# Two output projections from eight products to seven, with operand sums kept in DRAM

## The chip, the core and the metric

The kernel runs on one core of one Trainium2 chip. The metric is device time in microseconds, the median of several runs. A core has TensorE (PE, matmuls; PEld is its weight load), VectorE (DVE), ScalarE (ACT), GpSimd (POOL) and SyncE (SP). DMAs are issued from the queues of SP, GpSimd and (once, here) ScalarE.

## The reference

One layer of a decoder block over x of 2048 tokens by 1024 channels, all in float32. Cut to what matters here:

```python
h = rms_norm(x, norm_g)
v_c, b_c, c_c, z_c, q, k, v, z_a, gate_logits = split(h @ w_in)      # 1024 -> 8704 columns
y_c = b_c * conv3(c_c * v_c) * silu(z_c)         # causal, depthwise, width 3
y_a = y_c @ w_conv_out                           # 1024 x 1024
o = sliding_window_attention(rms(q), rms(k), v, sinks) * silu(z_a)   # window 128, 16 heads, 4 kv heads
y_b = o @ w_attn_out                             # 1024 x 1024
g_a, g_b = split(sigmoid(gate_logits + gate_b))
out = x + (g_a * y_a + g_b * y_b) @ w_out        # 1024 x 1024
```

## The kernel before

**Layout and precision.** The work is done in two tiles of 1024 tokens (`NT` = 2, `T` = 1024), with channels on the partitions. Every float32 operand is split into a high part, rounded to the format that TensorE multiplies in, and a low part, the rest. The high part is a cast on ScalarE, the low part a subtraction on VectorE (`split`, L240, for operands; `two`, L308, for weights; VectorE's operations all carry L213, the line of the helper that issues them). A product of two operands takes three matmuls: high x high, high x low, low x high. A matmul has a 128 x 128 weight block and 512 columns.

**Seven products.** A unit is a block of 256 output columns over one tile. The inner dimension is halved (1024 channels as 4 pairs of chunks of 128), the tokens are halved (q = 0, 1) and the output columns are halved (i = 0, 1), so a unit is a 2 x 2 block product. `sunit` computes it with seven products in place of eight, with sums of weights and sums of operands formed beforehand, and a few sums of results afterwards. `product` (L412) issues one of the seven: 4 x 3 = 12 matmuls. The order is 1, 5, 6, 2, 7, 3, 4. Results gather in three PSUM banks, X, V and Y. Between products ScalarE copies X into Y and V into a spare buffer s5, and VectorE adds; then a function `fin` takes each of the four quarters away (gate, store, multiply).

**The operands.** The seven operands of the tile's h, in 4 chunks each, are 28 buffers of the pool `oppool`, which has just 28. All input projections use them: k, v, q, cv (the convolution's two inputs), b, the merge gates ga and gb, and the gates za and z. In the first tile k and v go another way, and the first q unit too.

**The two branch projections.** `ya_unit` and `yb_unit` did not use seven products. After z, 16 operands of the gated convolution output were split straight from SBUF (`opa`), and 16 of the gated attention output were loaded back from the DRAM tensor `ocd` (`ocr`, then `opb`). `mm_t` (L1154) multiplied them in the plain way: for each quarter of a unit 8 chunks x 3 matmuls. VectorE took a quarter from PSUM, multiplied it by the gate (`tha`, `thb`, loaded from `gd`) and stored it: ya's to `md`; yb's was added to `m`, loaded back from `md`, and the sum went to `mt`, from which the output projection loaded its operand as weights. During yb the operands of the next tile (`next_tile`), or of w_out (`wo_side`), were loaded, normalized, summed in SBUF and split.

**What sets the order.** Each engine's instructions run in the order in which they are recorded, by a hand-made clock of ticks: a tick is one product (12 matmuls, in the plain projection a half quarter). `put(n, f)` sets a step to be recorded at tick n; `run` goes through a unit product by product and records, at each tick, weight loads (`ahead_loads`), one piece of the next weights (`piece`) and the steps due. Weights: raw loads of 512 KB, up to four at once; their split forms take a ring of 8 buffers, of which a unit of seven products needs 7. Attention blocks (32 per tile) are placed by a list of ticks; each has steps from its loads at 5 ticks ahead to its sum at 15 ticks after. Small buffers of 128 x 512 come from a pool of 19 (`slot`), wider ones from a pool of 2 (`upool`).

Of the kernel before, what the change touches and what calls it, by code (L numbers as in the profile page):

```python
# [8 lines left out]
F32 = mybir.dt.float32  # L9
# [49 lines left out]


@with_exitstack
def block_kernel(
# [37 lines left out]
    def bank(name):  # L100
        return ps_x.tile([P, H], F32, tag="x", name=name)
# [16 lines left out]
    ocd = [dram.tile([KC, P, T], F32, name=f"ocd{t}") for t in range(NT)]  # L118
    yd = [dram.tile([KC, P, T], F32, name=f"yd{t}") for t in range(NT)]
    md = [dram.tile([KC, P, T], F32, name=f"md{t}") for t in range(NT)]  # L120
    mt = [dram.tile([KC, P, T], F32, name=f"mt{t}") for t in range(NT)]
# [132 lines left out]
    WRING, RAWS = 8, 4  # L254
    live, rawlive = [0], [0]

    def load_half(i=None):
# [16 lines left out]
        elif kind in "SP":  # L274
# [8 lines left out]
        else:  # L283
            raw = rawpool.tile([P, KP, UC], F32, tag="raw", name=name)
            w, c0 = srcs
            nc.sync.dma_start(raw, w[c0 // UC, h].rearrange("r (j c) -> r j c", c=UC))
# [12 lines left out]
    def pieces_of(n):  # L299
# [15 lines left out]
        if kind in "SP":  # L315
# [9 lines left out]
            def single():  # L325
                hl = wpool.tile([P, 2, KP, P], F32R, tag="w", name=f"{name}_d")
                w[4] = (hl[:, 0], hl[:, 1])
                return two(hl[:, 0], hl[:, 1], raws[2 * n + 1][:, 1])
# [19 lines left out]
            return w, [(2, 0, lambda: pair(0, 1, 2, "a")), (1, 0, single), (0, 0, sums),  # L348
                       (2, 1, lambda: of_sums(1, 5, 6, "s")), (2, 1, lambda: of_sums(0, 7, 3, "t"))]

        def part(p):
            hi, lo = (v.rearrange("p (j c) -> p j c", c=UC) for v in wpair(f"{name}_{p}"))
            w[p] = (hi, lo)
            return two(hi, lo, raws[2 * n + p])

        return w, [(2, 1, lambda: part(0)), (2, 1, lambda: part(1))]

    def open_prep():
# [3 lines left out]
        w, pieces = pieces_of(n)  # L362
        ready.append(w)
        todo.extend((n, i) + p for i, p in enumerate(pieces))
        return True

    def piece():
# [4 lines left out]
        need = [2 * n + i] if plan[n][0] in "TP" else [2 * n, 2 * n + 1][: 1 + min(i, 1)]  # L372
# [24 lines left out]
    Y = ps_y.tile([P, H], F32, tag="y", name="Y")  # L397
# [8 lines left out]
    def product(ps, u, n, ops, start):  # L406
# [11 lines left out]
        live[0] -= sum(c for m, c in USES if n in m and m <= d)  # L418
# [4 lines left out]
    def sunit(key, ops, fin, two=False):  # L423
# [34 lines left out]
    def qunit(key, ops, fin):  # L458
# [4 lines left out]
        for q in range(2):  # L463
            for i in range(2):
                ps = bank(f"Q{nm}_{i}_{q}")
# [545 lines left out]
    def att_values(t, j, b, pcv, v2):  # L1011
        xh, xl, y = pcv
        po = mbank(f"po{t}_{j}_{b}").rearrange("p g q -> p (g q)")
        for h in range(2):
            cs = slice(h * 2 * P, (h + 1) * 2 * P)
            for n, (kind, xx) in enumerate(((2 + h, xh), (h, y), (2 + h, xl))):
                nc.tensor.matmul(  # L1017
                    po[:, cs], lhsT=v2[:, kind, :], rhs=xx[:, :, h * HD : (h + 1) * HD],
                    start=n == 0, stop=n == 2)
# [89 lines left out]
    def fin_z(t, j, src, nm, use):  # L1109
        other = {}  # L1110

        def load():
            for i, q in ((0, 0), (1, 1), (0, 1), (1, 0)):
                o = slot([P, H], F32, f"{nm}in{t}_{j}_{i}_{q}")
                nc.sync.dma_start(o, src[2 * j + i, :, hs(q)])
                other[i, q] = o

        def fin(i, q, val):
# [7 lines left out]
            def last():  # L1126
                o = other[i, q]
                mul(o, o, s)
                use(k, q, o)
# [7 lines left out]
        return fin, load  # L1137

    def split_op(src, name):
        o = optile(name)  # L1140
        split(o[:, 0], o[:, 1], src)
        return o


    def mm_t(ps, u, half, opt, q, first, last):
        cs = slice(half * P, (half + 1) * P)

        for n, k in enumerate((0, 2, 4, 1, 3, 5, 6, 7) if first else (0, 2, 4, 6, 1, 3, 5, 7)):
            j, p = divmod(k, 2)
            force(u, p)  # L1150
            hi, lo = ready[u][p]
            o = opt[k, q]
            for i, (w, m) in enumerate(((hi, 0), (hi, 1), (lo, 0))):
                nc.tensor.matmul(  # L1154
                    ps, lhsT=w[:, j, cs], rhs=o[:, m, :],
                    start=n == 0 and i == 0, stop=n == KC - 1 and i == 2)
            if n == KP - 1:
                live[0] -= 2 * last
                yield
        live[0] -= 2 * last  # L1160

    def quarters(order):
        return [(hf, q) for q in order for hf in range(2)]

    def branch(t, key, j, opt, fin, order):
        u = unit((key, t, j))
        for n, (hf, q) in enumerate(quarters(order)):
            ps = bank(f"{key}{t}_{j}_{hf}_{q}")
            yield from mm_t(ps, u, hf, opt, q, (key, j) == ("ya", 0), n == 3)
            fin(2 * j + hf, q, ps)  # L1170
            yield

    def load(src, k, q, name):
        tl = slot([P, H], F32, name)
        nc.sync.dma_start(tl, src[k, :, hs(q)])
        return tl

    def ya_unit(t, j, opt, order):
        th = {}

        def get(n):
            for hf, q in quarters(order)[2 * n : 2 * n + 2]:
                k = 2 * j + hf
                th[k, q] = load(gd[t][0], k, q, f"tha{t}_{k}_{q}")

        def fin(k, q, ps):
            m = th[k, q]
            vec.scalar_tensor_tensor(
                out=m, in0=m, scalar=1.0, in1=ps, op0=ALU.add, op1=ALU.mult)
            nc.sync.dma_start(md[t][k, :, hs(q)], m)  # L1190

        return branch(t, "ya", j, opt, fin, order), get

    def yb_unit(t, j, opt, order):
        th, m1 = {}, {}

        def get(n):
            pair = upool.tile([P, 2 * H + 2], F32, tag="u", name=f"thb{t}_{j}_{n}")
            for i, (hf, q) in enumerate(quarters(order)[2 * n : 2 * n + 2]):
                k = 2 * j + hf  # L1200
                th[k, q] = pair[:, hs(i)]
                nc.sync.dma_start(th[k, q], gd[t][1][k, :, hs(q)])
                m1[k, q] = spare(f"m1{t}_{k}_{q}")
                nc.sync.dma_start(m1[k, q], md[t][k, :, hs(q)])

        def fin(k, q, ps):
            m = th[k, q]
            vec.scalar_tensor_tensor(
                out=m, in0=m, scalar=1.0, in1=ps, op0=ALU.add, op1=ALU.mult)
            add(m, m, m1[k, q])  # L1210
            nc.sync.dma_start(mt[t][k, :, hs(q)], m)

        return branch(t, "yb", j, opt, fin, order), get
# [22 lines left out]
    def wo_side(n0, st):  # L1236
        raw = st["raw"]

        def ld(c):
            for q in range(2):  # L1240
                h = raw[c, q] = slot([P, H], F32, f"wo_{c}_{q}")
                nc.gpsimd.dma_start(h, w_o[c * P : (c + 1) * P, hs(q)])  # L1242

        def sums(j):
# [445 lines left out]
```

## Time and profile before

| | |
|---|---|
| median of 3 runs | 1946.24 us (1945.74 to 1947.4) |
| profiled execution: span | 1944.5 us; its own time outside the trace is not given apart, and the median is 1.7 us above the span |
| PE busy, matmuls | 1929.3 us, 99%, 8846 |
| DVE busy | 1462.6 us, 75% |
| ACT busy | 937.8 us, 48% |
| POOL busy | 580.9 us, 30% |
| DMA | 366.54 MB, 189 GB/s over the span |

A share of busy time is a mean over stages with different limits. In the span, the first tile's projections and attention run to about 572 us, za and z to 729, ya to 816 and yb to 905; the second tile has the same stages up to 1788, and the output projection follows. The page's rows in tenths cut the span into 40 slices. The chain of waits goes back from the last instruction: at each step to what released it.

### The profile page before, as it was taken

How to read it: one execution, taken by the hardware profiler on the slowest of the kernel's cores; microseconds unless marked ns; L12 is line 12 of the kernel's file. 1: busy time of each engine (PE TensorE's matmuls, PEld its weight loads, DVE VectorE, ACT ScalarE, POOL GpSimd, SP SyncE). 2: the span in 40 equal slices, each digit the busy share in tenths (PEclk: the TensorE clock that was granted, in tenths of full speed). 3: DMA queues.
4: the chain of work that ended last, by engine and by line, in shares of the span. 5: the costliest groups of instructions: out<-in, count | busy, mean ns of one | idle time of the engine just before them, and what ended most of it. 6: DMA issues, size and time to landing. Idle time of an engine off the chain costs nothing.

```text
span 1944.5 us, 27473 instructions
## 1 busy us (share of the span) xinstructions
PE 1929.3 (99%) x8846; PEld 1602.0 (82%) x8846; DVE 1462.6 (75%) x2500; ACT 937.8 (48%) x1876; POOL 580.9 (30%) x826
## 2 busy tenths in 40 slices
PE   9999999999999999999999999999999999999999
PEld 7778888888888888888878888888888888888887
DVE  7999898888886564379689888888997664366654
ACT  7655455556664342224565544556675343222221
POOL 2361443445662000100462343445654000100000
PEclk9999999999999999999999999999999999999999
DMA  8485555577775435874585554577776435855453
GB/s 306 104 217 172 153 162 170 165 224 235 236 248 190 168 97 184 291 246 136 161 207 156 167 163 142 164 224 234 238 236 213 167 109 183 283 180 171 152 174 113
DMA packets 217375, 366.54 MB, mean 189 GB/s; under 512 B 29264, under 2 KB 104016, under 8 KB 217232
## 3 DMA queue, kind: packets, MB, share of 16 engines
q1 hardware_dynamic: 189696, 288.96, 46.8%
q0 software_dynamic: 27392, 75.80, 13.5%
q8 instruction: 70, 1.15, 0.2%
q14 instruction: 73, 0.60, 0.1%
q10 hardware_dynamic: 144, 0.03, 0.0%
HBM read 251.17 MB, written 113.51 MB: 188 GB/s over the span
## 4 chain that ended last, share of the span: by engine, by line
PE 86%; DVE 7%; DMA 3%; issue 2%; POOL 2%; ACT 1%; SPq 0%; DVEq 0%; POOLq 0%
PE Y L412 27%; PE yb L1154 9%; PE ya L1154 8%; PE Vcv L412 4%; PE Xcv L412 4%; PE Xgb L412 2%; PE Vgb L412 2%; PE Xza L412 2%; PE Vza L412 2%; PE Vga L412 2%; PE Xz L412 2%; PE Vo L412 2%; PE Xo L412 2%; PE po L1017 2%; PE Xga L412 2%
## 5 line engine op out<-in xcount | busy, mean ns | idle before, releaser
L979 POOL DMA_DIRECT2D x<-fd x256 | 139.6, 551 | 92.7 <-DMA fd<-f 57.5
L1000 POOL TENSOR_SCALAR_AFFINE_SELECT xh<-xh 64x512 fp32r<-64x512 f32 x64 | 72.9, 1140 | 139.4 <-DVE xl L213 122.8
L952 ACT ACTIVATE p<-s,st,rq 128x128 f32<-128x128 f32 x256 | 112.9, 450 | 0.0
L972 POOL DMA_DIRECT2D fd<-f x64 | 37.0, 578 | 246.6 <-DVE f L213 215.9
L213 DVE SCALAR_TENSOR_TENSOR tha<-tha,ya 128x512 f32<-128x512 f32 x32 | 22.0, 687 | 96.3 <-PE ya L1154 96.3
L1154 PE MATMUL ya<-opa,wya_1h 128*128 128x512 f32 x256 | 79.5, 391 | 0.9 <-ACT opa L240 0.5
L412 PE MATMUL Xcv<-oph,wcv_ah 128*128 128x512 f32 x256 | 79.5, 392 | 0.0
L1154 PE MATMUL yb<-opb,wyb_1h 128*128 128x512 f32 x256 | 78.9, 389 | 0.0
L1154 PE MATMUL yb<-opb,wyb_0h 128*128 128x512 f32 x256 | 78.9, 389 | 0.0
L1154 PE MATMUL ya<-opa,wya_0h 128*128 128x512 f32 x256 | 78.8, 389 | 0.0
L240 ACT CAST opb<-ocr 128x512 fp32r<-128x512 f32 x32 | 19.9, 621 | 111.3 <-DMA ocr<-ocd 106.0
L1000 POOL TENSOR_SCALAR_AFFINE_SELECT xl<-xl 64x512 fp32r<-64x512 f32 x64 | 68.6, 1072 | 4.4
L1242 POOL DMA_DIRECT2D wo<-in_w_out x16 | 8.7, 541 | 192.6 <-DVE opb L213 180.5
L521 POOL DMA_DIRECT2D x<-in_x x8 | 4.3, 539 | 202.6 <-PE ya L1154 201.8
L1154 PEld LDWEIGHTS ya<-opa,wya_1h 128*128 128x128 f32 x256 | 48.1, 188 | 12.2 <-ACT opa L240 1.3
L1000 POOL TENSOR_SCALAR_AFFINE_SELECT yp<-yp 64x512 fp32r<-64x512 f32 x64 | 56.4, 881 | 4.2
L1154 PEld LDWEIGHTS ya<-opa,wya_0h 128*128 128x128 f32 x256 | 48.1, 188 | 10.0
L1154 PEld LDWEIGHTS yb<-opb,wyb_1h 128*128 128x128 f32 x256 | 48.0, 188 | 10.0
L1154 PEld LDWEIGHTS yb<-opb,wyb_0h 128*128 128x128 f32 x256 | 48.0, 188 | 9.9
L1000 POOL TENSOR_SCALAR_AFFINE_SELECT yp<-xl 64x512 fp32r<-64x512 f32 x64 | 54.8, 857 | 3.1
L308 ACT CAST wcv_sh<-wcv_raw 128x1024 fp32r<-128x1024 f32 x16 | 16.9, 1055 | 80.3 <-DVE wcv_raw L213 80.3
L412 PEld LDWEIGHTS Xcv<-oph,wcv_ah 128*128 128x128 f32 x256 | 47.4, 188 | 9.5
(591 smaller groups left out, 6376.7 us busy)
## 6 DMA issues: line engine op xcount, KB each, us to landing
wcv_raw<-in_w_in SPq DMA_DIRECT2D x32, 512.0 KB, 4.1
q<-q2d SPq DMA_DIRECT2D x64, 256.0 KB, 4.1
fd<-f POOLq DMA_DIRECT2D x64, 256.0 KB, 3.9
v<-vd SPq DMA_DIRECT2D x128, 128.0 KB, 3.4
x<-fd POOLq DMA_DIRECT2D x256, 64.0 KB, 3.1
gd<-th SPq DMA_DIRECT2D x64, 256.0 KB, 2.9
wq_raw<-in_w_in SPq DMA_DIRECT2D x16, 512.0 KB, 5.3
q2d<-q_h POOLq DMA_DIRECT2D x64, 128.0 KB, 4.6
```

The lines of the kernel that those rows point to most:

```text
L213: r = f(*args, **kw)
L240: nc.scalar.copy(hi, src)
L308: return (lambda: nc.scalar.copy(hi, src), lambda: vec.tensor_tensor(out=lo, in0=src, in1=hi.bitcast(F32), op=ALU.subtract))
L412: nc.tensor.matmul(ps, lhsT=w[:, j, :], rhs=b[:, m, :], start=start and j == 0 and i == 0, stop=j == KP - 1 and i == 2, skip_group_check=n ...
L521: eng.dma_start(xt, x2[r0 : r0 + P, :])
L952: nc.scalar.activation(out=p[:, i, :], in_=sg[:, i, HD : 3 * HD], func=AF.Exp, bias=st[:, 1, i : i + 1], scale=rv[:, i // 2, i % 2 : i % 2 ...
L972: nc.gpsimd.dma_start(fd, f)
L979: nc.gpsimd.dma_start(x[QUADS[k]], src[k])
L1000: nc.gpsimd.affine_select(out=d4, in_=s4, pattern=[[0, 2], [-32 * sg, 2], [0, G], [-sg, 32]], compare_op=ALU.is_gt if prev else ALU.is_ge, ...
L1017: nc.tensor.matmul(po[:, cs], lhsT=v2[:, kind, :], rhs=xx[:, :, h * HD : (h + 1) * HD], start=n == 0, stop=n == 2)
L1154: nc.tensor.matmul(ps, lhsT=w[:, j, cs], rhs=o[:, m, :], start=n == 0 and i == 0, stop=n == KC - 1 and i == 2)
L1242: nc.gpsimd.dma_start(h, w_o[c * P : (c + 1) * P, hs(q)])
```

## The change

**Seven products for ya and yb.** The units ya and yb go through `sunit`, with weights laid out and summed like all others. Their operands are three more sets of 28: "c" (gated convolution), "a" (gated attention) and, as before, the next tile's h or w_out.

**Sums in DRAM.** The sums of a set are formed early and stored: `fin_z` multiplies by the gate, stores three of four quarters (`ycd`, `ocd`), and `sums_of` makes four sums on VectorE and stores them in `sd`. The next tile's norms and sums (`h_stats`, `h_prep`) and w_out's (`w_prep`) are made the same way, at ticks spread over earlier stages. `load_set` then loads the 28 chunks of a set, in the order of the products, 3 ticks ahead of their splits. DMAs for za's results, for h and for w_out are issued by GpSimd, for z's results by SP.

**Pairs at seams.** Where one set gives way to the next, two units run product by product in turn (`paired_units`, `both`): the last two of za, all of ya and yb, the first two ga units of the second tile and the first two of the output projection. The second unit's X, V and Y lie in the banks of the pool `ps_m`. In a paired unit the weights of product 4 take two small buffers and not one of the ring.

**Order.** z now comes before za. In the second tile two ga units come first. The ticks of the attention blocks are given as two lists (`AT0`, `AT1`).

**Accumulating.** yb's gated quarters are added to `md` by a DMA that accumulates in DRAM, issued by GpSimd; the load of `m`, the add and `mt` are gone.

```diff
+ORDER = (1, 5, 6, 2, 7, 3, 4)
+PAIR_PIECES = ((0, 0), (0, 1), (1, 0), (1, 1), (0, 2), (1, 2), (0, 3), (1, 3))
+SUM_AT = {5: 0, 6: 1, 7: 2, 4: 3}
+RAW_AT = {1: (0, 0), 2: (1, 0), 3: (1, 1)}
+SET_AHEAD, Z_AHEAD, Y_AHEAD = 3, 3, 3
+SET_STEP = 3
+H_AT = (11, 25, 66, 81)
...
-    def sunit(key, ops, fin, two=False):
+    def sunit(key, ops, fin, two=False, other=False):
+        bank = flat_bank if other else x_bank
         xb = bank(f"X{nm}")
         product(xb, u, 1, ops, True)
+        Y = flat_bank(f"Y{nm}") if other else Y0
         nc.scalar.copy(Y, xb)
...
+    def sums_of(key, j, r, n0, eng):
+        def first():
+            sub(r[0, 0], r[0, 1], r[0, 0])
+            eng.dma_start(sd[key][0, j], r[0, 0])
+            sub(r[0, 1], r[1, 1], r[0, 1])
+            eng.dma_start(sd[key][2, j], r[0, 1])
+        def second():
+            sub(r[1, 1], r[1, 1], r[0, 0])
+            eng.dma_start(sd[key][1, j], r[1, 1])
+            sub(r[1, 0], r[1, 0], r[1, 1])
+            eng.dma_start(sd[key][3, j], r[1, 0])
+        put(n0, first)
+        put(n0 + 1, second)
...
+    def load_set(key, n0, ops):
+        for idx, m in enumerate(ORDER):
+            for jj in range(2):
...
+                def ld(m=m, jj=jj, src=src, got=got):
+                    if jj == 0:
+                        pair = upool.tile([P, 2 * H + 2], F32, tag="u", name=f"in{nm}_{m}_{jj}")
+                        got.extend(pair[:, hs(i)] for i in range(2))
+                        nc.sync.dma_start(
+                            pair[:, 0 : 2 * H].rearrange("p (j x) -> p j x", j=2),
+                            src.rearrange("j p x -> p j x"))
+                    else:
+                        for i in range(2):
+                            got.append(slot([P, H], F32, f"in{nm}_{m}_{jj}_{i}"))
+                            nc.sync.dma_start(got[i], src[i])
+                def put_in(i, m=m, jj=jj, got=got):
+                    o = new_op(nm, m, 2 * jj + i, ops)
+                    split(o[:, 0], o[:, 1], got[i])
+                n = n0 + SET_STEP * idx + 2 + jj
+                put(n - SET_AHEAD, ld)
+                for i in range(2):
+                    put(n, lambda i=i, f=put_in: f(i))
...
+    def fin_y(t, w, j, at_of):
...
+            val = plain(val, f"{nm}p{t}_{k}_{q}")
             vec.scalar_tensor_tensor(
+                out=m, in0=m, scalar=1.0, in1=val, op0=ALU.add, op1=ALU.mult)
+            if w:
+                nc.gpsimd.dma_start(md[t][k, :, hs(q)], m, accum_op=ALU.add)
+            else:
+                nc.sync.dma_start(md[t][k, :, hs(q)], m)
...
+    def both(a, b):
+        for _ in a:
+            yield
+            next(b)
+            yield
...
+        load_set(("c", t), tick[0] + 1, opa)
+        n = tick[0] + 1
+        paired_units([
+            (("za", t, j), ops, za(j, lambda e, i=i, n=n: n + 2 * e + i))
+            for i, j in enumerate(range(NJ - 2, NJ))])
+        for w, key, o in ((0, "ya", opa), (1, "yb", opb)):
+            for j in range(0, NJ, 2):
+                if (w, j) == (0, NJ - 2):
+                    load_set(("a", t), tick[0] + 1, opb)
+                if (w, j) == (1, NJ - 2):
+                    nxt = ("h", t + 1) if t + 1 < NT else ("w", 0)
+                    load_set(nxt, tick[0] + 1, x_state(t + 1)["ops"])
+                n = tick[0] + 1
+                paired_units([
+                    ((key, t, j + i), o, fin_y(t, w, j + i, lambda e, i=i, n=n: n + 2 * e + i))
+                    for i in range(2)])
```

More of the change, by code (lines that the diff above doesn't have):

```diff
@@ L1135, in fin @@
                 gate(val)
[L1137 to L1176, printed above, removed]
@@ L1194, in yb_unit @@
[L1194 to L1213, printed above, removed]
+        return fin
@@ L1566, in block_kernel, with paired_units @@
+    def paired_units(units):
+        (ka, oa, fa), (kb, ob, fb) = units
+        run(both(sunit(ka, oa, fa), sunit(kb, ob, fb, other=True)))
     tick0 = 0
@@ L1626, in block_kernel @@
[L1626 to L1638 removed]
+        if t + 1 < NT:
+            h_stats(t + 1, tick[0] + 2)
```

377 lines of the change are left out of this document (202 added, 175 removed).

## The prediction

> **What bounds the kernel now.** I read the page first, then who TensorE waited for, then the chain of waits in order of time, the groups by form, and at last the busy time and the DMA by stretch.
>
> ```profile
> span 1944.5 us, 27473 instructions
> ...
> PE 1929.3 (99%) x8846; PEld 1602.0 (82%) x8846; DVE 1462.6 (75%) x2500; ACT 937.8 (48%) x1876; POOL 580.9 (30%) x826
> ...
> DVE  7999898888886564379689888888997664366654
> ...
> PE 86%; DVE 7%; DMA 3%; issue 2%; POOL 2%; ACT 1%; SPq 0%; DVEq 0%; POOLq 0%
> ```
>
> TensorE is busy in every slice of the span (at the full clock, by the rows of stretches below), and the chain that ended last runs 86% through it. Whether that is work or waiting inside a busy row is told by the waits of TensorE, longest first (13 rows in all):
>
> ```profile
> PE ptr L536 <- DVE rtok L530: 1.7, 1, 1.7
> ...
> PE Vq L412 <- ACT q_t L505: 1.4, 1, 1.4
> PE Vq L412 <- DVE wq_sl L213: 1.2, 2, 0.7
> PE Vcv L412 <- DVE wcv_sl L213: 1.2, 3, 0.5
> ...
> PE ya L1154 <- ACT opa L240: 0.5, 2, 0.2
> PE ya L1154 <- DVE opa L213: 0.4, 2, 0.2
> ```
>
> Thirteen rows of at most 1.7 us are under 22 us of 1944.5, and the two seams from the gates z to the branch projections cost 0.9 us together, or 0.45 us each. So the kernel is a queue of matmuls, and its time is their number times their pace. The pace, from the chain in order of time (start, length, what):
>
> ```profile
> 860.88 43.55 PE yb L1154 x192
> ...
> 1701.02 87.04 PE yb L1154 x384
> ...
> 1788.06 2.72 PE Xo L412 x12
> ```
>
> Both ways of multiplying run at one pace: 87.04 / 384 = 0.2267 us in the plain projection, 2.72 / 12 = 0.2267 us in a product of seven. I call 2.72 us, one product, a step.
>
> **What is removed.** ya and yb have 384 matmuls each per tile, 1536 in all. By seven products each of the 16 units (two branches, two tiles, four blocks of 256 output columns) has 7 x 4 x 3 = 84, together 1344. The built program has 8656 matmuls where it had 8848: 192 fewer. The chain has a row for just that many: 192 x 0.2267 = 43.5 us (43.55 as seen). TensorE lies on the path from end to end, so all of it counts unless something else comes late.
>
> **What is added on the other engines.** Counted in the built programs, VectorE gets 192 more operations of 512 columns (48 operand splits, 64 weight sums, 16 weight splits, 64 operand sums; 32 adds in the units take the place of the 32 that joined the branches) and 16 more weight splits of 1024. ScalarE gets 48 more operand casts, 32 PSUM copies and 16 weight casts, all of 512, and 16 casts of 1024; GpSimd 132 more DMAs. Their prices, by group (count, busy us, mean ns, idle before):
>
> ```profile
> L213 DVE TENSOR_TENSOR opb<-ocr,opb 128x512 fp32r<-128x512 f32 x32 | 21.9, 688 | 6.9 <-ACT opb L240 6.8
> L213 DVE TENSOR_TENSOR wyb_0l<-wyb_raw,wyb_0h 128x1024 fp32r<-128x1024 f32 x8 | 9.7, 1218 | 0.0
> L213 DVE SCALAR_TENSOR_TENSOR thb<-thb,yb 128x512 f32<-128x512 f32 x32 | 21.9, 685 | 42.4 <-PE yb L1154 41.4 <-DMA thb<-gd 0.6
> L240 ACT CAST opb<-ocr 128x512 fp32r<-128x512 f32 x32 | 19.9, 621 | 111.3 <-DMA ocr<-ocd 106.0 <-PE ya L1154 5.3
> L308 ACT CAST wyb_0h<-wyb_raw 128x1024 fp32r<-128x1024 f32 x8 | 8.4, 1050 | 33.3 <-issue 17.5 <-PE yb L1154 12.9 <-PE ya L1154 2.9
> L561 POOL DMA_DIRECT2D h<-in_xt x16 | 8.6, 537 | 10.3 <-DMA h<-in_xt 3.2 <-DVE wyb_0l L213 2.3 <-DVE wyb_1l L213 1.6
> L213 DVE TENSOR_TENSOR wq_raw<-wq_raw,wq_raw 128x512 f32<-128x512 f32 x9 | 6.2, 687 | 0.1
> L213 DVE TENSOR_TENSOR wgb_raw<-wgb_raw,wgb_raw 128x512 f32<-128x512 f32 x12 | 8.3, 692 | 0.4
> L213 DVE TENSOR_TENSOR wgb_raw<-wgb_raw,wgb_raw 128x512 f32<-128x512 f32 x6 | 5.8, 959 | 0.1
> ```
>
> VectorE: 192 x 0.688 + 16 x 1.218 = 152 us more, 1615 of some 1901 us (85%). ScalarE: 96 operations of 512 x 0.621 + 16 x 1.050 = 76 us, to 1014 (53%). GpSimd: 132 x 0.537 = 71 us, to 652 (34%). None is the bound over the whole span; what matters is the stage. There the trace had room (length, then busy us of PE, PEld, DVE, ACT, POOL, clock, DMA share, GB/s):
>
> ```profile
> 60.00:130.00 70.00, 65.86 (x307) 52.64 (x306) 66.89 (x135) 43.28 (x75) 40.39 (x62) 1.00 0.63 156
> 400.00:572.00 172.00, 172.00 (x837) 145.33 (x836) 143.39 (x270) 115.37 (x281) 101.85 (x135) 1.00 0.79 239
> ...
> 729.00:905.00 176.00, 175.53 (x777) 144.59 (x776) 105.19 (x192) 50.58 (x76) 12.89 (x24) 1.00 0.67 229
> 1613.00:1788.00 175.00, 174.55 (x769) 144.03 (x768) 87.98 (x124) 41.42 (x59) 8.66 (x16) 1.00 0.64 208
> ```
>
> The last two rows are the stages of ya and yb; VectorE stood at 60% and 50% there. Afterwards I take the five alternating pairs of a tile (the last za pair, two of ya, two of yb), 5 x 14 steps = 190.4 us. The built program puts 170 + 39 operations of 512 and 30 of 1024 on VectorE there in tile 0 (the next tile's norms and sums among them): 209 x 0.688 + 30 x 1.218 = 180 us, 95%. In tile 1, 193 and 30: 169 us, 89%. ScalarE has 110 x 0.621 + 30 x 1.050 = 100 us, 53%. So VectorE just fits. The second row shows TensorE never waiting beside 83% on VectorE, the first at 96% with 94% of TensorE's own time, in the start of the kernel.
>
> **GpSimd's DMAs beside VectorE.** The last three rows of the groups are one kind of operation, a weight sum, in three stretches. From 60 to 130 us GpSimd is 58% busy, nearly all of it issuing DMAs for q, k and v: 687 ns. From 400 to 572 it is 59% busy, with the attention's selects: 692 ns. From 1374 to 1420, in the same stage of tile 1, the sums take 959 ns, 39% more; the work on GpSimd is of the same kind and only meets them at other moments. In the pairs GpSimd has no selects and issues DMAs, so I take the first row's price.
> [...]
>
> **Operand sets through DRAM.** A set of seven operands fills all 28 operand buffers. A buffer comes free when the pair's second unit has used that product, so at a seam new operands come in every 3 steps while the old ones leave every 2. The next pair needs product i (0 to 6) 14 + 2i steps after the pair began; its last split is recorded at 3i + 3. That leaves 11 - i steps, 5 (13.6 us) at the tightest. Loads are recorded 3 steps (8.2 us) ahead of the splits, on SP, where they queue behind stores that wait for VectorE; behind them stand the gates' and weights' loads, for which VectorE and ScalarE wait. The DMA at the change from ya to yb in tile 0, what loads took in the ya stages (tile 1, then tile 0), and how long ScalarE waited for one:
>
> ```profile
> GB/s 411 417 412 404 388 384 389 387 409 409 299 15 212 306 192 87 266 295 306 225 74 262 347 31 139 215 25 345 308 128 18 147 265 285 18 249 103 145 218 111
> ...
> ocr<-ocd SPq DMA_DIRECT2D x16, 256.0 KB, 4.2
> thb<-gd SPq DMA_DIRECT2D x2, 256.0 KB, 11.1
> ...
> ACT opb L240 <- DMA ocr<-ocd: 106.0, 27, 7.5
> ```
>
> The first row is 816 to 905 us in 40 slices of 2.2 us: loads and stores together held 384 to 417 GB/s for ten slices. The built program moves 63 MB in tile 0's five pairs (an accumulate counted as two passes) and 58 MB in tile 1's: 333 and 303 GB/s over 190.4 us, against 229 and 208 before. At 400 GB/s that is 158 and 145 us of DMA: not the bound, but at yb's start in tile 0 about 8.6 MB fall into five steps (13.6 us) and need 21.5, so loads there land some 8 us late. A load that took 4.2 us then takes 12, as thb's 11.1 did. TensorE's cover is 13.6 us and the weights split two steps ahead.
> [...]
>
> The price of a seam is not in the trace. Below, the old seams' 0.45 us; above, the longest wait of ScalarE for a load, 7.5 us, taken whole by TensorE. There are six now (z-to-ya, ya-to-yb and yb-to-next in each tile, where two had shown waits): 2.7 to 45 us. I take 1 us each, 6 in all, near the lower end because the splits have 5 to 11 steps of cover and ScalarE is at 53%. If that cover is gone, the upper end holds.
>
> The alternation gives each copy and add of a unit one more step before its bank is needed, and TensorE issues the same products: nothing. Accumulating into DRAM takes the place of a load, an add (0.69 us) and a store. Its duration isn't shown: from a load's 4.2 us to a load as late as thb's 11.1, the add and a store of the same length, 23. The output projection needs tile 0's result a tile later and tile 1's first 28 steps (76 us) after the last one: nothing, up to 76 us. Behind an accumulate in GpSimd's queue stand only loads and stores for the next operand set, whose sums are recorded 7 steps ahead of their loads. The attention blocks' new places and the first ga pair move work between stretches that VectorE nearly fills either way (q and conv, whose three rows of waits above make 3.8 us): 0, with 3.8 us either side.
>
> **The sum.** The profiled execution has a span of 1944.5 us; the median is 1.7 us above it, and I carry that along. 1944.5 - 43.5 + 6 = 1907.0; with 1.7, 1908.7.
>
> **Rivals.** *Late operands (26%).* At each seam ScalarE holds its queue for a late load, and TensorE pays 2 to 6 us: 1946.2 - 43.5 + 6 x (2 to 6) = 1915 to 1939. For it: 95% on VectorE, bursts over 400 GB/s; against: 5 steps of cover.
> *VectorE becomes the bound (4%).* If half of its operations in the pairs grow by 39%, as wgb's from 692 to 959, all take 20% more; tile 0's pairs take 216 us and tile 1's 203: 26 + 13 us, 1942, still just ahead. It decides from 5% growth on. Against it: the 687 ns beside DMA issues. [...]
> *DRAM traffic becomes the bound (13%).* The pairs' 121 MB go at no more than R. Up to 318 GB/s nothing is lost over both stages together (121 / 318 = 381 us); at 285 the gain is eaten up (425 us). The attention stage moved 239 GB/s at a share of 0.79, so 303 at full share; if mixed stores, loads and accumulates hold only 270, the pairs take 448 us, 67 more: 1970, slower. Against it: 384 to 417 GB/s held for 22 us in this very stage.
> That the matmuls don't go away can't be: they are counted.
>
> **How the numbers follow.** The forecast has 55% (1900 to 1915, below by the old waits and the runs' scatter). Late operands 26%, VectorE 4%, DRAM 13%, and 2% for a loss that just cancels the gain. A measurement tells some 0.2%, 3.9 us, from no change. Faster: 0.55 + 0.26 + 0.04 = 0.85; same 0.02; slower 0.13. The range 1900 to 1940 holds the forecast and late operands.
>
> **What would show it.** Right: 8654 or so matmuls, TensorE still 99% of a span near 1905, waits of TensorE for the operand splits of a few us in all, VectorE 1615 us busy, the pairs at 190 us each tile. Wrong: rows where a product waits for an operand split or for weights, tens of us long, ScalarE waiting for its loads at the same time (late operands); VectorE without idle time and means above 688 ns (VectorE); DMA at 9 throughout the pairs with landings above 12 us (DRAM).

## The result, and the profile after

The changed kernel takes 1932.04 us (1931.93 to 1932.86), beside 1946.44 us for the kernel before: a ratio of 0.9925, 95% interval 0.9911 to 0.9939. It is faster by 14.4 us, where 37.5 were forecast. The profiled execution (1932.86 us, span 1931.1) is read against that of before (span 1944.5).

The page first: the span, the busy times, and TensorE and VectorE by slices.

```profile
span 1931.1 us, 28062 instructions
...
PE 1894.6 (98%) x8654; PEld 1571.8 (81%) x8654; DVE 1596.3 (83%) x2708; ACT 1001.4 (52%) x1990; POOL 656.1 (34%) x958
...
PE   9999999999999999999998999999999999999999
...
DVE  7989999889888888878577899889888878886654
```

The 192 matmuls are gone (8654 for 8846), but TensorE's busy time fell by 34.7 us, not 43.5, and its idle time rose from 1944.5 - 1929.3 = 15.2 us to 36.5. So 1944.5 - 43.5 + 21.3 of idle time + 8.8 of slower matmuls = 1931.1. By the clock's records TensorE worked 16.3 us at half clock, half of which is 8.1 of the 8.8. One slice of PE, the 22nd (1014 to 1062 us), shows an 8. Who TensorE waited for (total us, times, longest):

```profile
PE Y L443 <- DVE Vq L233: 11.1, 2, 7.7
PE s L959 <- ACT p L988: 4.8, 1, 4.8
PE Vya L443 <- ACT zas L1219: 2.0, 1, 2.0
PE Vyb L443 <- DVE thya L233: 1.9, 1, 1.9
```

The first two rows are neither at a seam nor in a branch projection. They are q units of the second tile (Vq is one of q's PSUM banks) and the attention's scores (s). The stretches of 5 us around them (length, busy us of PE, PEld, DVE, ACT, POOL, granted clock, DMA share, GB/s), and the matmuls at which TensorE went on (the waits in brackets):

```profile
1005.00:1010.00 5.00, 1.79 (x8) 1.13 (x7) 4.91 (x8) 1.75 (x4) 5.00 (x9) 0.94 0.88 231
1010.00:1015.00 5.00, 4.78 (x11) 3.84 (x12) 4.78 (x8) 3.69 (x6) 3.08 (x5) 0.50 0.94 283
...
1035.00:1040.00 5.00, 0.00 (x0) 0.00 (x0) 4.86 (x13) 2.23 (x4) 4.76 (x8) 0.67 0.78 163
1040.00:1045.00 5.00, 4.95 (x15) 3.97 (x16) 4.78 (x8) 3.29 (x6) 2.79 (x5) 0.65 0.77 243
```

```profile
1010.22 1.22 PE L443 MATMUL Y<-oph,wq_th 128*128 128x512 f32 x2 [3.43 <-DVE Vq L233]
...
1040.05 1.22 PE L443 MATMUL Y<-oph,wq_th 128*128 128x512 f32 x2 [7.68 <-DVE Vq L233]
...
1077.55 0.62 PE L959 MATMUL s<-lows,kq 128*128 128x384 f32 x1 [4.78 <-ACT p L988]
```

From 1010 to 1015 us TensorE is busy for 4.78 of 5 us and gets 11 matmuls done where a full stretch (1045 to 1050) has 24: the clock is at 0.50. Behind the three waits shown (3.43, 7.68 and 4.78 us) it works at half clock for 6.0, 3.5 and 3.4 us, so each of them cost more than its length. What VectorE itself waited for between 983 and 1045 us:

```profile
DVE wo L233 <- DMA wo<-in_w_out: 6.6, 2, 5.2
DVE q_l L233 <- DMA kd<-k_l: 3.9, 1, 3.9
...
DVE k_l L233 <- DMA q2d<-q_h: 2.8, 1, 2.8
```

wo is `w_prep`, the sums of w_out for the output projection, which the change records in the second tile's k, v and q units; the other two wait for stores that still hold a buffer of the shared pool `big`. The longest of these waits ends 7.6 us before TensorE goes on at 1040.05, with more sums and q's own steps in between:

```profile
1032.44 0.69 DVE L233 TENSOR_TENSOR wo<-wo,wo 128x512 f32<-128x512 f32 x1 [5.17 <-DMA wo<-in_w_out]
...
1039.31 0.68 DVE L233 TENSOR_TENSOR Vq<-s5q,Y 128x512 f32<-128x512 f32 x1
```

The whole stretch 980 to 1110 us, before and after:

```profile
980.00:1110.00 130.00, 128.97 (x578) 105.46 (x577) 116.41 (x233) 70.45 (x141) 55.05 (x81) 1.00 0.61 167
```

```profile
980.00:1110.00 130.00, 113.18 (x482) 92.36 (x481) 104.52 (x213) 67.74 (x129) 75.58 (x117) 0.93 0.79 223
```

(The program runs a little earlier after the change, so the stretches hold nearly but not exactly the same work; the loss is the idle time, 16.8 us against 1.0, and the clock.) The stages of the seams lose much less. The five pairs of each tile, from the first matmul of the last za pair to the end of yb, after:

```profile
694.70:892.90 198.20, 193.38 (x842) 158.41 (x841) 167.25 (x240) 91.45 (x141) 33.31 (x55) 0.99 0.89 294
1584.50:1774.90 190.40, 190.40 (x841) 157.71 (x840) 156.81 (x225) 91.54 (x141) 21.36 (x33) 1.00 0.85 276
```

The second tile's pairs take just the 190.4 us of the prediction, the first tile's 7.8 us more.

### The profile page after: what moved, and what is told of

The parts are those of the page before. It is cut to its first block, busy times and chain, and to the rows that moved or that the text cites. A ratio compares the mean times of both kernels' runs of the same rounds, so it can differ in the third digit from the quotient of the medians.

```text
span 1931.1 us, 28062 instructions
## 1 busy us (share of the span) xinstructions
PE 1894.6 (98%) x8654; PEld 1571.8 (81%) x8654; DVE 1596.3 (83%) x2708; ACT 1001.4 (52%) x1990; POOL 656.1 (34%) x958
## 4 chain that ended last, share of the span: by engine, by line
PE 79%; DVE 8%; DMA 6%; issue 4%; POOL 1%; ACT 1%; SPq 0%; DVEq 0%; POOLq 0%; ACTq 0%
PE Y L443 28%; PE Vcv L443 5%; PE Xcv L443 4%; PE Xgb L443 2%; PE Vgb L443 2%; PE Xb L443 2%; PE Vb L443 2%; PE Xz L443 2%; PE Vz L443 2%; PE Vo L443 2%; PE Xo L443 2%; PE po L1053 2%; PE Vza L443 2%; PE Xza L443 2%; PE Vga L443 2%
## 5 line engine op out<-in xcount | busy, mean ns | idle before, releaser
L233 DVE TENSOR_TENSOR o<-po,o 64x256 f32<-64x256 f32 x128 | 53.4, 417 | 1.6 <-ACT o L1065 0.5
L233 DVE TENSOR_TENSOR opa<-ina,opa 128x512 fp32r<-128x512 f32 x56 | 36.1, 686 | 22.0 <-ACT opa L260 21.9
L233 DVE SCALAR_TENSOR_TENSOR y<-u,cols,y 128x512 f32<-128x512 f32 x64 | 51.1, 799 | 2.9 <-ACT y L1102 1.7
L810 POOL DMA_DIRECT2D q2d<-q_h x64 | 44.3, 692 | 24.5 <-ACT q_h L805 20.0
L325 ACT CAST wcv_sh<-wcv_raw 128x1024 fp32r<-128x1024 f32 x16 | 16.9, 1055 | 68.1 <-DVE wcv_raw L233 62.7
L233 DVE TENSOR_TENSOR p<-p,st 128x512 f32<-128x512 f32 x64 | 48.9, 764 | 3.3
L988 ACT ACTIVATION_READ_ACCUMULATOR p<-s,st,rq 128x1 f32 x256 | 50.6, 198 | 0.0
L810 POOL DMA_DIRECT2D q2d<-q_l x64 | 44.1, 689 | 19.1 <-DVE q_l L233 8.5
L443 PE MATMUL Xcv<-oph,wcv_al 128*128 128x512 f32 x128 | 49.8, 389 | 0.0
L1065 ACT COPY o<-po 64x256 f32<-64x256 f32 x128 | 47.1, 368 | 5.2 <-PE po L1053 3.0
L233 DVE TENSOR_TENSOR opc<-inc,opc 128x512 fp32r<-128x512 f32 x56 | 36.2, 686 | 15.8 <-ACT opc L260 15.8
```

The costliest lines, as they stand in the source:

```text
L233: r = f(*args, **kw)
L325: return (lambda: nc.scalar.copy(hi, src), lambda: vec.tensor_tensor(out=lo, in0=src, in1=hi.bitcast(F32), op=ALU.subtract))
L443: nc.tensor.matmul(ps, lhsT=w[:, j, :], rhs=b[:, m, :], start=start and j == 0 and i == 0, stop=j == KP - 1 and i == 2, skip_group_check=n ...
L810: nc.gpsimd.dma_start(q2d[t][j][half, q * 2 * HB : (q + 1) * 2 * HB, i, e, :], src[HALVES[e]].bitcast(F32).rearrange("p (b x) -> p b x", x ...
L988: nc.scalar.activation(out=p[:, i, :], in_=sg[:, i, HD : 3 * HD], func=AF.Exp, bias=st[:, 1, i : i + 1], scale=rv[:, i // 2, i % 2 : i % 2 ...
L1065: nc.scalar.copy(ov, pov[oth, :, e])
```

## The experiments

Three theories were set against each other at first. A: `w_prep` in the second tile's k, v and q units makes the stalls, and the halved clock behind them is part of the price. B: the second tile's attention comes too early for its k, v and q. C: operands come late at the seams.

**w_prep in the z units.**

```diff
-        if t + 1 == NT:
-            w_prep(tick[0] + 1, W_STEP)
...
         if t + 1 < NT:
             h_prep(t + 1, tick[0])
+        else:
+            w_prep(tick[0] + 1, W_STEP)
```

> The changed kernel (1932.0 us), with the sums of w_out prepared during the second tile's gates z and za and not during its k, v and q. Theory A (w_out's 32 DMAs on GpSimd's queue and the sums that wait for them hold VectorE, and through it TensorE, among k, v and q; the clock is halved after each of those stalls): the stalls of 3.4 and 7.7 us and the 6.8 us lost to the halved clock behind them go, the stall of 4.8 us at the attention's scores may stay: 1914, from 1907 to 1918. Theory B (k, v, q and the attention stand too close in the second tile whatever else is there: earlier attention blocks after two ga units): the stalls stay, 1928 to 1934. Theory C (the loss is at the seams, from late operands, as the prediction's first rival had it): 1928 to 1934, since no seam is touched.

Measured 1926.76 us (1923.78 to 1928.07), ratio 0.9897 [0.9882, 0.9912], 5.3 us below the changed kernel: between the two. TensorE's waits:

```profile
PE s L959 <- ACT p L988: 6.1, 1, 6.1
PE Y L443 <- DVE zs L233: 5.1, 2, 4.1
```

The wait for Vq is gone, and the stretch 980 to 1110 us holds 122.66 us of matmuls instead of 113.18. But the scores' wait stays, and a new one stands where the sums now are. Between the same products (first matmul of q to the first of the conv units, first of z to the first of za) the q stage takes 82.0 us instead of 97.6, and z 89.1 instead of 81.9. A is right for q, and what is won there is half paid back in z.

**w_prep's DMAs by SP.** In `w_prep` `nc.gpsimd` became `nc.sync`, at the same place.

> The changed kernel, with the preparation of w_out's sums at its old place, but its 16 loads and 16 stores issued by SP and not by GpSimd. Theory A, with GpSimd's queue as the cause: VectorE no longer waits for the loads, 1907 to 1920. Theory A, with the VectorE work or the DMA traffic itself as the cause, or theory B or C: no change, 1928 to 1936.

Measured 1932.06 us (1929.95 to 1935.2): nothing. The wait for Vq is 10.8 us. It is not GpSimd's queue; the sums themselves and the DMA traffic stay open.

**Attention later as a whole.** `a0 = t0 + (14 if t else 0)` became `t0 + (20 if t else 0)`.

> The changed kernel, with the second tile's attention blocks all 6 ticks later and everything else at its place. Theory A: only the stall at the scores (4.8 us, 1.7 us of slow clock) can go: 1925 to 1931. Theory B (attention too close behind q): the stalls among q go too: 1905 to 1918. Theory C: 1928 to 1934.

Measured 1950.85 us, 18.8 us slower than the changed kernel. The wait for Vq stays (11.2 us) and the last blocks run into the z units (zs, 5.7 us), which take 13.7 us longer. B in this form falls.

**No accumulating DMA.** yb loads what ya left, adds on VectorE and stores.

```diff
-                nc.gpsimd.dma_start(md[t][k, :, hs(q)], m, accum_op=ALU.add)
+                add(m, m, m1[i, q])
+                nc.sync.dma_start(mt[t][k, :, hs(q)], m)
```

> The changed kernel, with the second branch joined as before the change: the first branch's quarter is loaded, added on VectorE (32 adds of 0.69 us) and the sum stored to a second tensor, and no DMA accumulates. If the accumulation costs nothing that shows and VectorE has the room that the forecast gave it (95% in the first tile's pairs): 1932 to 1936. If VectorE is full there: 1937 to 1950, with TensorE waiting for VectorE in the pairs. If the accumulating DMA itself is what delays the pairs' loads: 1920 to 1930.

Measured 1946.15 us (1941.4 to 1950.82): the whole gain is gone, 14.1 us. New rows of TensorE's waits:

```profile
PE Vo L444 <- DVE thyb L234: 4.2, 1, 4.2
PE Vga L444 <- DVE thyb L234: 3.5, 1, 3.5
PE Y L444 <- DVE ybp L234: 2.2, 1, 2.2
```

The first two are at the ends of the second and the first tile's yb, the third in the first tile's first yb pair. VectorE at the end of the first tile's yb, in this run and then in the changed kernel, from 873 us until it has caught up:

```profile
873.00:906.50 33.50, 30.00 (x133) 24.57 (x132) 32.95 (x48) 12.84 (x20) 0.00 (x0) 1.00 0.93 319
```

```profile
873.00:898.70 25.70, 25.70 (x115) 21.29 (x114) 25.42 (x37) 11.39 (x18) 5.98 (x7) 1.00 0.94 283
```

VectorE is full there in both (32.95 of 33.5 and 25.42 of 25.7 us) and waits for no load. With one more add in each quarter it catches up 7.8 us later, and TensorE waits for it: the second of the three cases. So one small addition at the end of yb costs a lot, and the change as made stays just below that.

**Attention's second block apart.** The changed kernel has the second tile's first two score blocks two products apart. Here `w_prep` is in z and `AT1` begins 40, 45 instead of 40, 42.

> Same as the kernel with w_prep moved to the second tile's z units (1926.76 us), and the second attention block of the second tile three products later (places 40, 45 instead of 40, 42). Theory A (the remaining loss is made of single stalls, each with a stretch at half clock behind it): the wait of the scores for ScalarE's exponentials (6.1 us there) goes, and with it about 3.4 us of half clock; 1916 to 1919 us. Theory D (ScalarE is late in that stage whatever the place, and the stall only moves to the next block): 1924 to 1928 us.

Measured 1924.8 us (1917.59 to 1926.57). The scores' wait is gone from the rows; small ones took its place (Y for ScalarE's copy, 4.1 us in four, Vcv for a weight split, 2.9 in two). By the median D is right, but the trace gives it only half: the second tile's stages from k to the gates take 554.0 us, 2.9 less than with `w_prep` in z alone, while the first tile's ga units, which the edit doesn't touch, take 2.4 more. One run of the four took 1917.59 us, so the median alone doesn't decide between A and D.

**w_prep spread like h_prep.** As before, but `w_prep` has the places that `h_prep` has in the first tile, over z, za and the pairs.

```diff
-            put(n0 + step * j, ld)
-            sums_of(("w", 0), j, r, n0 + step * j + 4, nc.gpsimd)
+            put(n0 + step[j], ld)
+            sums_of(("w", 0), j, r, n0 + step[j] + 4, nc.gpsimd)
...
+            w_prep(tick[0] + 1, H_AT)
```

> Attention's second block as in the run beside it (40, 45), and w_prep spread over z, za and the pairs of the second tile at the places that h_prep has in the first tile (11, 25, 66, 81 products after the start of z). Theory A: the wait for zs (5.1 us in two pieces, plus up to 6.8 us at half clock) goes too; 1908 to 1913 us, about the forecast. Theory D (the pairs of the second tile have no room on VectorE for the sums): the stall comes back at a seam, 1917 to 1926 us.

Measured 1918.42 us (1915.3 to 1921.35), ratio 0.9854 [0.984, 0.9869]. No wait of TensorE is over 2.0 us any more. The pairs of the second tile had the room.

**Scores close together in the first tile.** `AT0` begins 51, 53 instead of 51, 56, in the changed kernel.

> The changed kernel with one edit in the first tile, which has no stall there: its second attention block is put two products behind the first instead of five (51, 53 instead of 51, 56), as it is in the second tile. Theory A (two score blocks two products apart hold TensorE for the exponentials of the first, and the clock is halved after the stall): a wait of 4 to 6 us of the scores for ScalarE near the start of the first tile's conv units, a granted clock of 0.5 for 3.4 to 6.8 us behind it, 1938 to 1943 us. Theory D (it is the crowd of the second tile's q stage, not the spacing): no such wait, 1931 to 1934 us.

Measured 1935.21 us (1933.52 to 1938.47), 3.2 above. There is no wait of the scores for ScalarE in the first tile (0.9 us, put down to issue). The spacing alone doesn't stall TensorE; what makes it stall in the second tile is something else in that stage. A falls here. Of the profile's 2.9 us, 1.8 lie in the first tile's conv stage, in no wait that stands out; the rest isn't explained.

**A seam without alternation.** In both tiles the last two ya and first two yb units run one after the other.

```diff
-                n = n0 + SET_STEP * idx + 2 + jj
+                n = n0 + set_step * idx + (2 + jj if set_step > 1 else 5 + jj)
...
+                if (w, j) in ((0, NJ - 2), (1, 0)):
+                    for i in range(2):
+                        if (w, i) == (0, 1):
+                            load_set(("a", t), tick[0] + 1, opb, 1)
+                        n = tick[0] + 1
+                        run(sunit((key, t, j + i), o, fin_y(t, w, j + i, lambda e, n=n: n + e)))
+                    continue
```

> The changed kernel with the seam from the conv branch's to the attention branch's projection run as four single units instead of two alternating pairs, in both tiles; the next operand set is formed one group of eight splits per product during the last single unit and the first of the next branch, each group one product ahead of its use. Theory P (alternation is what gives VectorE and the freed buffers the time): 28 splits of 0.68 us on VectorE within some 8 products of 2.72 us, beside the weights' work, so 5 to 20 us more at each of the two seams with half clock behind the stalls; 1942 to 1975 us. Theory Q (alternation buys little, VectorE catches up from work done ahead): 1930 to 1938 us.

Measured 1968.06 us (1964.31 to 1971.75): 36 us more, and slower than the kernel before. Between the same products the first tile's yb takes 17.9 us longer and the second's 15.4. The waits are the operands (opa), as theory P has it:

```profile
PE Y L443 <- DVE opa L233: 9.5, 10, 3.0
PE Y L443 <- ACT opa L260: 4.3, 4, 1.6
```

and around the seam (840 to 880 us) the clock stands at 0.84. The next set's loads and splits are recorded later here than in pairs, so that both belong to the price. An earlier form, with the splits three products sooner, gave no time: its instructions wait for each other in a ring.

**Holding TensorE on purpose.** To the best version so far (1918.42 us) five holds are added in the calm start of the second tile:

```diff
+    def hold(k):
+        pt = mbank(f"hold{k}")
+        nc.tensor.transpose(pt[:, 0, :], ident, ident)
+        s = slot([P, P], F32, f"held{k}")
+        for _ in range(k):
+            nc.scalar.copy(s, pt[:, 0, :])
+        nc.tensor.transpose(pt[:, 1, :], s, ident)
```

> The best version so far (1918.42 us: w_prep at the places of h_prep, attention's second block at 45) with five holds of growing length put into the calm start of the second tile (3, 8, 13, 18 and 23 products in): a transpose, 1, 3, 6, 12 or 24 small ScalarE copies of its result one after the other, and a transpose of the copy, so that TensorE stands still for the copies. It does no work that the output needs. Estimate of the holds: some 0.6 us each plus 0.2 us per copy, 12 us in all. Theory A (each stall over some length halves the granted clock for a few us behind it, at a cost of about half of that time): clock records of 0.5 behind the long holds only, and 4 to 10 us above the holds' own sum, 1934 to 1941 us. Theory F (the low clock seen in the second tile's q stage has another source than the stalls): full clock behind all holds, 1927 to 1932 us.

Measured 1947.79 us (1944.5 to 1954.51), 29.4 above. The copies took longer than estimated (0.265 us each), so the holds came to 20.4 us of waiting and some 3 us of transposes. The first, of one copy, stood for 4.02 us, since its copy began only 3.7 us after the transpose. The waits by their hold, and the granted clock in the 4 us behind each:

```profile
903.40 0.33 PE L1642 MATMUL hold<-ident,held 128*128 128x128 f32 x1 [4.02 <-ACT held L1641]
...
922.38 0.33 PE L1642 MATMUL hold<-ident,held 128*128 128x128 f32 x1 [1.97 <-ACT held L1641]
...
938.78 0.33 PE L1642 MATMUL hold<-ident,held 128*128 128x128 f32 x1 [2.31 <-ACT held L1641]
...
957.37 0.47 PE L1642 MATMUL hold<-ident,held 128*128 128x128 f32 x1 [4.51 <-ACT held L1641]
...
983.01 0.48 PE L1642 MATMUL hold<-ident,held 128*128 128x128 f32 x1 [7.56 <-ACT held L1641]
```

```profile
903.00:907.00 4.00, 3.54 (x9) 2.69 (x10) 0.42 (x1) 0.34 (x2) 0.00 (x0) 0.61 1.06 380
922.00:926.00 4.00, 3.62 (x17) 2.99 (x18) 1.51 (x3) 0.29 (x2) 0.00 (x0) 1.00 0.27 108
939.00:943.00 4.00, 4.00 (x19) 3.31 (x19) 0.00 (x0) 0.69 (x1) 0.00 (x0) 1.00 0.71 246
957.00:961.00 4.00, 3.63 (x9) 2.93 (x10) 0.00 (x0) 0.28 (x2) 0.00 (x0) 0.50 0.00 0
983.00:987.00 4.00, 3.99 (x13) 3.23 (x14) 0.00 (x0) 0.90 (x1) 0.00 (x0) 0.65 0.02 4
```

Behind the holds of 1.97 and 2.31 us the clock is full; behind 4.02, 4.51 and 7.56 it is halved, for 3.4, 4.5 and 2.8 us by the clock's records (903.85 to 907.26, to 961.88 and to 985.77 us). Half of those 10.7 us is lost: 5.3, and with the holds' 23.4 that is 28.7 of the 29.4. Theory A of the clock stands, and over these three holds the loss didn't grow with the length.

**Attention's start, evenly and later.** On the same version `AT1` begins 45, 49, 53, 57, 61, 65, 70, 75, 80 instead of 40, 45, 51, 53, 59, 63, 68, 75, 80.

> The best version so far (1918.42 us) with the second tile's first nine attention blocks at 45, 49, 53, 57, 61, 65, 70, 75, 80 instead of 40, 45, 51, 53, 59, 63, 68, 75, 80; the rest stay. Theory G (attention begins while the last q unit's evacuations are still on ScalarE and VectorE, and the small waits of that stage, 4.4 us, come from there): 1913 to 1917 us. Theory D (the stage is full on VectorE anyhow, 116 of 130 us): 1917 to 1921 us.

Measured 1915.28 us (1914.17 to 1917.0), ratio 0.9841 [0.9827, 0.9856]: the fastest version, 31 us below the kernel before. The stretch of the second tile's start has no loss left:

```profile
980.00:1110.00 130.00, 128.94 (x578) 104.93 (x578) 116.92 (x232) 76.08 (x151) 67.73 (x101) 1.00 0.75 200
```

**w_prep's sums later.** In the changed kernel the sums stand 7 products behind the loads instead of 4.

> The changed kernel with w_prep where it is (the second tile's k, v and q units), but each group's sums seven products behind its loads instead of four (19.0 instead of 10.9 us). Theory H (VectorE takes its instructions in order and stands before sums whose loads land late; TensorE's wait for Vq is the work queued behind): the wait for wo (6.6 us) goes and most of the wait for Vq (11.1 us) with it, 1920 to 1926 us. Theory J (it is the buffers: four of nineteen held for longer hold up the loads of the weights and everything behind them on the DMA queues): the stall stays or grows, 1931 to 1940 us.

Measured 1929.75 us (1929.1 to 1936.61). VectorE's wait for wo fell to 0.5 us and TensorE's for Vq left the rows, but others came, and the stretch still lost most of its time (115.77 us of matmuls):

```profile
PE s L959 <- DMA lows<-kd: 4.1, 1, 4.1
PE Y L443 <- DVE q_t L233: 3.6, 2, 2.6
PE s L959 <- ACT p L988: 2.9, 1, 2.9
```

So H names the wait rightly but not the limit, and the median lies in neither theory's range. With the wait for wo gone, the scores wait for loads of k's low part (lows from kd), and the q stage still takes 96.8 us, against 97.6.

One more candidate was not tried. The q stage before, and in the changed kernel (the last two numbers are the DMA engines' share and GB/s):

```profile
946.00:1026.00 80.00, 79.49 (x357) 64.45 (x356) 65.96 (x121) 47.61 (x81) 54.22 (x83) 1.00 0.82 212
```

```profile
972.00:1070.00 98.00, 85.96 (x368) 69.28 (x367) 75.28 (x136) 47.92 (x82) 66.75 (x105) 0.93 0.85 241
```

The DMA engines are busy for 0.82 x 80 = 66 us of it before and 0.85 x 98 = 83 us after, about as much more as the stage grew, and as full as ever. That the transfers of `w_prep` and not its sums are what hold the stage is possible and not shown; a run with its loads and stores but without its sums would tell.

**Attention's start alone.** The new `AT1` in the changed kernel, `w_prep` where it was.

> The changed kernel with the later and evener start of the second tile's attention (45, 49, 53, 57, 61, 65, 70, 75, 80) and nothing else: w_prep stays in the k, v and q units. It is the fourth corner of a square with the changed kernel (1932.04 us), w_prep moved (with block 2 at 45: 1918.42 us) and both moved (1915.28 us). Theory A (w_prep's sums make the q stage's long wait by themselves): the wait for Vq (11.1 us) stays, the wait of the scores for ScalarE goes, 1923 to 1930 us. Theory B (two causes of which either is enough, so that taking away attention's early start clears the stage): no wait over 2 us there, 1915 to 1920 us.

Measured 1929.31 us (1928.42 to 1929.9): the wait for Vq stays at 11.6 us, the scores' goes, 2.7 us better. The q stage takes 95.9 us, against 97.6. Theory A holds at this corner, but the time is near its upper end.

## Why the prediction was right and wrong

The direction was right and the time lay within the range, but the gain was forecast 2.6 times too large. That the range holds the time is luck: its upper part was there for late operands at the seams, and the loss came elsewhere.

*The pace and the count.* Right: 192 matmuls fewer, and away from stalls the pace is the same, as the chain of waits of the changed kernel shows in its yb pairs (5.44 / 24 = 0.2267):

```profile
854.97 5.44 PE Xyb L443 x24
```

But I took the pace for fixed, and the matmuls behind the stalls took 8.8 us more.

*The work added.* The counts were right (208 more operations on VectorE). Its busy time grew by 133.7 us, not 152. Added up row by row it grew by 158.5, but neighbouring rows overlap, by 94 us in all before and 118 after, and busy time counts an overlap once (an operand split alone is 0.686 us). ScalarE ended at 1001.4 us (1014 forecast), GpSimd at 656.1 (652). The splits' 686 ns stand in stretches where GpSimd issues DMAs, so the row I took held, and VectorE as the bound did not come about.

*The pairs.* I had VectorE at 95 and 89% in them; it was at 84 and 82%, and DMA at 294 and 276 GB/s instead of 333 and 303. On the average they are less full than feared. But at the end of the first tile's yb VectorE works without a gap for 25.7 us, and the run with one more add per quarter, which makes that 33.5, lost 14 us: the mean over the pairs hides that.

*The seams.* 1 us each, 6 in all: TensorE's waits between 690 and 910 us make 5.2, and between 1550 and 1780 us 0.5, with some 1.7 us of slow clock. From the first matmul of the gates z and za to the end of yb the two tiles lose 7.4 and 0.8 us beyond the products removed. This term was nearly right, though not evenly spread, and the late operands did not come about. DRAM as the bound didn't either.

*Alternation and the accumulating DMA, priced at nothing.* No row of TensorE's waits names either. They are what the seams' low price rests on: without the first the two yb stages cost 17.9 and 15.4 us more, without the second the kernel loses 14 us.

*The step that failed* is the last before the sum, "the attention blocks' new places and the first ga pair ... 0, with 3.8 us either side". Here lie the two waits that I had bounded by three rows of before: 11.1 and 4.8 us, and 12.9 of the 16.3 us at half clock. I took these stages as nearly full on VectorE (116 of 130 us in the row of before, above) and then priced only what the change moves there among its own kind. I left out what it newly puts there: `w_prep`, four groups of four loads, four sums and four stores, in the stretch of the second tile with the least room. And the attention of the second tile begins 11 products earlier after the start of k than before (40 where it was 51). The term is measured between the same products (us, from the profiles). The column "k to the gates" runs from the second tile's first unit to its first of z (before: of za), with 2184 matmuls of units in each kernel:

| | q stage | k to the gates | z stage |
|---|---|---|---|
| before | 80.2 | 551.6 | |
| changed | 97.6 | 570.9 | 81.9 |
| `w_prep` in z | 82.0 | 556.9 | 89.1 |
| `w_prep` spread, second block three products later | 80.9 | 554.0 | 83.5 |
| attention's start alone | 95.9 | 567.9 | 81.9 |
| spread, and attention's start | 80.4 | 552.5 | 83.7 |

So the term was 19.3 us and not 0 with 3.8 either side. `w_prep` is most of it: taken away it gives back 14.0 to 16.9 us, attention's later start 3.0, and both 18.4, so the two about add up. With `w_prep` in z the whole gained only 5.3 us, since z then took 7.2 us more. What in `w_prep` holds the stage stays open. In the long wait VectorE stands before a load that lands late, as in my rival of late operands, but in a stage where I had not looked for it; and the run with later sums took that wait away and kept 16.7 of the 19.3 us, so it is not the limit by itself.

*The sum, mended.* The seams' stages took 8.2 us, the step that failed 19.3, and all the other stages, priced at nothing, 2.6: 1944.5 - 43.5 + 8.2 + 19.3 + 2.6 gives the span of 1931.1. In the fastest version, by the same points, it is 1944.5 - 43.5 + 8.1 + 1.0 + 2.4 = 1912.5. That is 5.5 us above the forecast's 1907.0: 2.1 more at the seams, 1.0 in the step that failed and 2.4 elsewhere. Which steps hold these was not tried.

## What to carry to other kernels

Where a queue of matmuls bounds a kernel, count what a change adds stage by stage, every helper by the tick at which it is recorded, and look first at the stages that are full already: the price lay not where the change was made but where its preparations were put. Look for what stands behind a stall, too: the six of 3.43 to 7.68 us above (three waits, three holds) had 2.8 to 6.0 us at half clock behind them, an estimated 1.4 to 3.0 us beyond their length, and the wait of 1.99 us had 3.4 us at half clock behind it in one profile and none in another. When a step is moved, measure between the same products both the stage that it leaves and the one that it enters: the time of the whole shows only the difference.

## What was not expected of the hardware

The granted clock was 0.50 behind the holds of 4.02, 4.51 and 7.56 us, for 3.4, 4.5 and 2.8 us, and stayed full behind those of 1.97 and 2.31 us. The length alone doesn't decide it. In the changed kernel a wait of 1.99 us that ended at 743.04 us had matmuls at half clock behind it, and in the run with `w_prep` in z one of the same length at the same place, ended at 742.78, had none. The clock's records show where the two differ. Within each profile the stretches at half clock, but for the one at the very end, are one to four times 3.413 us long and begin whole multiples of that apart (in the changed kernel at 743.14, 1009.38, 1036.68 and 1077.64 us: 78, 8 and 12 times). If intervals of 3.413 us are laid on from these starts, those around the two waits are, first the changed kernel, then the other:

```profile
739.73:743.14 3.41, 1.42 (x7) 0.85 (x5) 2.78 (x6) 2.37 (x5) 0.54 (x1) 1.00 0.54 170
743.14:746.55 3.41, 3.41 (x8) 2.65 (x9) 2.86 (x5) 3.04 (x7) 0.85 (x2) 0.50 0.79 226
746.55:749.97 3.42, 3.42 (x16) 2.82 (x15) 2.68 (x4) 2.21 (x5) 1.65 (x4) 1.00 1.03 344
```

```profile
739.16:742.57 3.41, 1.63 (x8) 1.02 (x6) 2.78 (x6) 2.06 (x4) 0.54 (x1) 1.00 0.55 148
742.57:745.98 3.41, 3.20 (x14) 2.67 (x15) 2.86 (x6) 3.15 (x7) 0.54 (x2) 1.00 0.86 240
```

In the first the wait lies whole in one interval, and the next one has a clock of 0.50. In the second an edge cuts it into 1.78 and 0.21 us, and the clock stays at 1.00. All 13 changed kernels profiled have this wait, of 1.98 or 1.99 us: in four it lies within one interval and the clock is halved, in nine an edge leaves at most 1.85 us in one, and it isn't. The edges cut the holds of 1.97 and 2.31 us too, into pieces of at most 1.51 us. So for these waits the clock went with how much of the wait fell into one interval; what sets it isn't shown.

yb's DMAs that accumulate in DRAM took GpSimd longer to issue than za's plain ones of the same 256 KB (874 against 542 ns, by the groups of the changed kernel), and landed as late as the loads beside them (7.1 and 7.2 us, by its DMA issues):

```profile
L1259 POOL DMA_DIRECT2D md<-thyb x32 | 27.4, 874 | 172.9 <-DVE thyb L233 165.0
...
L1226 POOL DMA_DIRECT2D ocd<-zain x24 | 13.0, 542 | 129.3 <-DVE zain L233 126.7
```

```profile
thyb<-gd SPq DMA_DIRECT2D x32, 256.0 KB, 7.2
md<-thyb POOLq DMA_DIRECT2D x32, 256.0 KB, 7.1
```
